# Context and latent tokens of a key or value block in one padded row, one instruction per tap of the short convolution

## The chip, the cores and the metric

The kernel runs on one core of a Trainium2 chip. The metric is the device time of one execution in microseconds (us). The time before is the median of three runs. One further execution was profiled; the rows shown below are from that one.

## The reference, cut to what matters

One layer of a hybrid backbone: a combined input projection feeds a gated DeltaNet (4 heads, 128 wide, for queries, keys and values) and a convolution module; then comes a mixture of experts. There are 1024 latent tokens and 256 context tokens. Before the DeltaNet, queries, keys and values go through a depthwise convolution over 7 tokens and a Silu. Context and latent are separate sequences for it, each padded with three zeros at both ends:

```python
def depthwise_conv_seq(x, w):
    k, ch = w.shape
    return lax.conv_general_dilated(x, w[:, None, :].astype(x.dtype), (1,), [(k // 2, k // 2)],
                                    dimension_numbers=('NWC', 'WIO', 'NWC'), feature_group_count=ch)

def delta_inputs(qkv, ba, conv_w, a_log, dt_bias):
    bsz, n, _ = qkv.shape
    qkv = jax.nn.silu(depthwise_conv_seq(qkv, conv_w)).astype(jnp.float32)
```

Queries of the context are never used by the output, so the kernel computes queries for the latent tokens alone.

## The kernel before, in words

A block is 128 channels of the projection, held with channels in the partitions and tokens along a row. There are 12 such blocks for the convolution: 0 to 3 are queries, 4 to 7 keys, 8 to 11 values. `qkv_block` (L550) makes one. It loads and splits the weights (`load_in`, L309; `split`, L290), then `fm` (L314) multiplies on TensorE into a PSUM bank of the ring "a" (4 banks): segment 0 is the 256 context tokens, segments 1 and 2 are 512 latent tokens each, 24 matmuls a segment. ScalarE copies the latent banks into the padded row `cx` (1030 wide, ring of two, L557) and, for keys and values, the context bank into a second padded row `cc` (262 wide, ring of two, L565). GpSimd writes the zeros at the ends (L554, L555, L563, L564).

`conv7` (L542) does the seven taps on a row: the first is a scaled copy on ScalarE (L546), the other six are fused multiply-adds on VectorE (L548), each of which reads the result of the one ahead of it. A key or value block calls it twice, for 1024 and for 256 columns. Keys are convolved straight into `kf`, values into `ac` (ring of two). One Silu over all 1280 columns follows (L569), then TensorE transposes ten chunks of 128 tokens (L573). For keys the squares are summed into `ssk` (L579, L580); the result goes to DRAM as `kv_d`.

What runs around it: the four key blocks come first; beside them the layer norm of the convolution module is finished (L469 to L488). Then `key_norms` (L661) needs the sums of all four key blocks. Then follow, for four pairs of chunks, `prep1` (L687: decay matrices and a product of keys, `wt`, stored to DRAM and fetched again in another layout through `bounce` into `rep`, one buffer), a value block, and `base_inverse` (L720: 15 steps, each a product `tm`, L730, and a sum `xf`, L731, on VectorE, that read `rep`). A fifth pair goes beside the query blocks. `conv_out` (L593) and `z_block` (L586) are further products; `sqq` (L766) and its matmul (L767) sum the squares of all four query blocks.

Each engine runs its own instructions in order. In this part of the program (up to L793) that order is made by the Tile framework when the program is built: it goes by the order in the source and by when it reckons an instruction to be ready, so that an engine's list mixes several blocks. From L793 on the order is planned by the kernel itself from fixed durations (`Order`, L86), and the change touches nothing there.

Of the kernel before, what the change touches and what calls it, by code (L numbers as in the profile page):

```python
# [8 lines left out]
F32 = mybir.dt.float32  # L9
# [3 lines left out]
AF = mybir.ActivationFunctionType  # L13
# [136 lines left out]
def hybrid_kernel(tc, a, out):  # L150
    nc = tc.nc
    V, S, G, PE, SY = nc.vector, nc.scalar, nc.gpsimd, nc.tensor, nc.sync
# [14 lines left out]
    def bank(tag, bufs=4, dt=F32, n=512):  # L167
        return pp.tile([128, n], dt, name=tag, tag=tag, bufs=bufs)

    def csl(c):  # L170
        return slice(c * 128, (c + 1) * 128)
# [51 lines left out]
    ident = cp.tile([128, 128], F32, name="ident")  # L223
# [15 lines left out]
    pt = bank("b")  # L239
# [69 lines left out]
    def load_in(c0):  # L309
        return load_w(win[:, :, c0:c0 + 128])  # L310
# [3 lines left out]
    def fm(wt, seg):  # L314

        t0, n = SEG[seg]
        ps = bank("a")
        for k in range(8):
            for i, (l, r) in enumerate(((wt[0], hTh), (wt[0], hTl), (wt[1], hTh))):
                PE.matmul(ps[:, :n], l[:, k, :], r[:, k, t0:t0 + n], start=(k == 0 and i == 0),  # L320
                          stop=(k == 7 and i == 2))
        return ps
# [3 lines left out]
    pt = bank("b")  # L326
# [69 lines left out]
    pt = bank("b")  # L396
# [35 lines left out]
    pt = bank("b")  # L432
# [19 lines left out]
    qf = keep2.tile([128, 4, 1024], F32, name="qf")  # L452
# [38 lines left out]
    kf = keep2.tile([128, 4, 1280], F32, name="kf")  # L491
# [37 lines left out]
    pt = bank("b")  # L529
# [10 lines left out]
    cvp = st_cv.enter_context(tc.tile_pool(name="cv", bufs=1, reuse_waits="tile"))  # L540

    def conv7(dst, src, blk, n):  # L542
        for t in range(7):
            wt = cnv[:, t * 12 + blk:t * 12 + blk + 1]
            if t == 0:
                S.activation(dst, src[:, 0:n], AF.Copy, scale=wt)  # L546
            else:
                V.scalar_tensor_tensor(dst, src[:, t:t + n], wt, dst, op0=OP.mult, op1=OP.add)  # L548

    def qkv_block(blk):  # L550
        wt = load_in(blk * 128)
        kind, h = divmod(blk, 4)
        cx = cvp.tile([128, 1030], F32, name="cx", bufs=2)
        G.memset(cx[:, 0:3], 0.0)  # L554
        G.memset(cx[:, 1027:1030], 0.0)  # L555
        for hf in range(2):
            S.activation(cx[:, 3 + hf * 512:3 + (hf + 1) * 512], fm(wt, 1 + hf), AF.Copy)  # L557
        if kind == 0:
            conv7(qf[:, h, :], cx, blk, 1024)
            S.activation(qf[:, h, :], qf[:, h, :], AF.Silu)  # L560
            return
        cc = cvp.tile([128, 262], F32, name="cc", bufs=2)
        G.memset(cc[:, 0:3], 0.0)  # L563
        G.memset(cc[:, 259:262], 0.0)  # L564
        S.activation(cc[:, 3:259], fm(wt, 0)[:, :256], AF.Copy)  # L565
        dst = kf[:, h, :] if kind == 1 else cvp.tile([128, 1280], F32, name="ac", bufs=2)
        conv7(dst[:, 256:1280], cx, blk, 1024)
        conv7(dst[:, 0:256], cc, blk, 256)
        S.activation(dst, dst, AF.Silu)  # L569
        for i0, nt in ((0, 4), (4, 4), (8, 2)):  # L570
            pt = bank("b")
            for t in range(nt):
                PE.transpose(pt[:, csl(t)], dst[:, csl(i0 + t)], ident)  # L573
            pv = pt.rearrange("p (t c) -> p t c", t=4)[:, :nt, :]
            ot = cvp.tile([128, 4, 128], F32, name="ot", bufs=2)
            if kind == 1:
                S.activation(ot[:, :nt], pv, AF.Copy)
                sq = cvp.tile([128, 4, 128], F32, name="sq", bufs=1)
                S.activation(sq[:, :nt], pv, AF.Square)  # L579
                V.tensor_reduce(ssk[:, i0:i0 + nt, h], sq[:, :nt], axis=AX.X, op=OP.add)  # L580
            else:
                V.tensor_tensor(ot[:, :nt], pv, rk[:, i0:i0 + nt, h][:, :, None].to_broadcast([128, nt, 128]),
                                op=OP.mult)
            SY.dma_start(kv_d[i0:i0 + nt, :, kind - 1, h].rearrange("t p c -> p t c"), ot[:, :nt])
# [155 lines left out]
    for h in range(4):  # L740
        qkv_block(4 + h)
    prp = st_cv.enter_context(tc.tile_pool(name="prep", bufs=1, reuse_waits="tile"))
    key_norms()
    for h in range(4):
        run_together([prep1(pairs[h])])
        qkv_block(8 + h)
        run_together([base_inverse(pairs[h])])
    for h in range(3):
        qkv_block(h)
        if h == 0:  # L750
            run_together([prep1(pairs[4])])
        if h == 1:
            run_together([base_inverse(pairs[4])])
# [7 lines left out]
    for hf in range(2):  # L761
# [8 lines left out]
        pt = bank("b")  # L770
# [1062 lines left out]
```

## Time and profile before

| | us |
|---|---|
| median of three runs | 1741.64 (1737.73 to 1743.6) |
| profiled execution | 1741.28 |
| its span in the trace | 1739.6 |
| PE busy | 1575.7 (91%) |
| DVE busy | 1001.3 (58%) |
| POOL busy | 537.5 (31%) |
| ACT busy | 494.5 (28%) |

PE is TensorE's matmuls, DVE VectorE, ACT ScalarE, POOL GpSimd, SP the queue that issues most transfers. Times in the trace count from the span's start. The blocks of the change lie between about 200 and 400 us. In the timelines an instruction's duration runs from its start until its result is there; the next instruction of the same engine can start before that, so start-to-start distances are read beside durations. "[4.18 <-DMA rep]" behind a row is idle time of the engine ahead of it and what ended it.

### The profile page before, as it was taken

The page shows a single profiled execution, that of the slowest core. Times are in us where ns is not written, and L with a number is a line of the kernel's source. Part 1 is how long each engine was busy: PE and PEld are TensorE (multiplying, and loading weights), DVE is VectorE, ACT ScalarE, POOL GpSimd, SP SyncE. Part 2 cuts the span into 40 slices and gives each one's busy share as a digit, 9 for nine tenths or more (in the row PEclk, how much of TensorE's full clock was granted, in tenths as well). Part 3 has the DMA queues.
Part 4 walks back from the last instruction along what each step waited for, and adds up shares of the span by engine and source line. Part 5 has one row for each costly group of instructions (what it writes and reads, how often), then busy time and mean ns, then how long its engine had stood idle before and what let it go on. Part 6 is the DMA issues. An engine that isn't in the chain of part 4 may idle for free. (4 is left out here: it accounts for less than half of the span.)

```text
span 1739.6 us, 23353 instructions
## 1 busy us (share of the span) xinstructions
PE 1575.7 (91%) x8348; PEld 924.7 (53%) x8348; DVE 1001.3 (58%) x2236; ACT 494.5 (28%) x1071; POOL 537.5 (31%) x486
## 2 busy tenths in 40 slices
PE   5989998876869899798999999999999999999990
PEld 1557667764647899687544434344444344433440
DVE  2488989889671886878712444444444444443425
ACT  4531266534122212444212121212121111121212
POOL 2321214543212677732011232323232222232212
PEclk8999999998889999899999999999999999999995
DMA  9455123434643334766358999999999999999956
GB/s 318 152 175 176 37 65 94 121 106 124 167 145 127 109 104 154 233 220 218 120 223 304 340 345 342 329 366 335 334 380 381 342 337 331 344 383 370 354 137 232
DMA packets 151112, 412.12 MB, mean 237 GB/s; under 512 B 19383, under 2 KB 66900, under 8 KB 125396
## 3 DMA queue, kind: packets, MB, share of 16 engines
q1 hardware_dynamic: 129994, 334.62, 53.3%
q0 software_dynamic: 18288, 67.05, 15.2%
q10 hardware_dynamic: 2714, 8.95, 1.3%
q8 instruction: 66, 1.08, 0.3%
q14 instruction: 50, 0.41, 0.1%
HBM read 339.48 MB, written 71.43 MB: 236 GB/s over the span
## 5 line engine op out<-in xcount | busy, mean ns | idle before, releaser
L1353 PE MATMUL gu<-wg,hg 128*32 128x512 f32 (+2 forms) x1968 | 463.2, 599 | 0.7 <-ACT hg L1604 0.7
L1629 DVE SCALAR_TENSOR_TENSOR ob<-dn,wc,gt2b 128x512 f32<-128x512 f32 x124 | 93.0, 750 | 366.0 <-PE dn L1373 366.0
L1638 POOL DMA_INDIRECT acc<-ob,ic x89 | 134.6, 1513 | 530.3 <-DVE st L1563 460.1
L1353 PEld LDWEIGHTS gu<-wg,hg 128*32 128x32 f32 (+2 forms) x1968 | 148.4, 137 | 203.2 <-issue 159.2
L1373 PE MATMUL dn<-wd,sg 128*32 128x512 f32 (+2 forms) x984 | 226.8, 597 | 0.5 <-ACT sg L1364 0.5
L1604 ACT ACTIVATE hg<-xt,mf 128x128 f32<-128x128 f32 x248 | 93.4, 456 | 376.4 <-PE xt L1598 375.9
L320 PE MATMUL a<-hTh,whi 128*128 128x512 f32 (+1 forms) x448 | 171.5, 383 | 3.7 <-ACT cx L557 3.7
L320 PE MATMUL a<-hTh,wlo 128*128 128x512 f32 (+1 forms) x448 | 170.3, 380 | 0.0
L320 PE MATMUL a<-hTl,whi 128*128 128x512 f32 (+1 forms) x448 | 170.3, 380 | 0.0
L1373 PEld LDWEIGHTS dn<-wd,sg 128*32 128x32 f32 (+2 forms) x984 | 77.8, 137 | 143.5 <-issue 142.7
L294 POOL TENSOR_TENSOR wlo<-wst,whi 128x512 fp32r<-128x512 f32 x56 | 82.3, 1487 | 214.3 <-ACT whi L293 209.7
L1602 DVE TENSOR_SCALAR hg<-xt,mf 128x128 f32<-128x128 f32 x248 | 84.3, 401 | 50.4 <-DMA acc<-hg 50.4
L427 DVE SCALAR_TENSOR_TENSOR ycv<-yg,cfw,ycv 128x64 f32<-128x64 f32 (+14 forms) x120 | 101.3, 844 | 6.1 <-ACT ycv L421 2.9
L320 PEld LDWEIGHTS a<-hTh,whi 128*128 128x128 f32 x448 | 84.8, 189 | 30.2 <-issue 9.9
L320 PEld LDWEIGHTS a<-hTh,wlo 128*128 128x128 f32 x448 | 85.0, 190 | 18.7 <-issue 3.4
L320 PEld LDWEIGHTS a<-hTl,whi 128*128 128x128 f32 x448 | 84.9, 189 | 18.0 <-issue 3.0
L1588 POOL DMA_INDIRECT xg<-xn_d,ig x62 | 74.1, 1195 | 64.9 <-DVE st L1583 28.3
L1552 DVE TENSOR_TENSOR oh<-posl 128x1024 bf16<-128x1024 f32 (+3 forms) x89 | 77.6, 897 | 0.0
L1598 PE MATMUL xt<-ident,xg 128*128 128x128 f32 x496 | 70.3, 285 | 0.0
L293 ACT ACTIVATE whi<-wst 128x512 fp32r<-128x512 f32 x56 | 33.0, 624 | 107.0 <-PE a L320 66.2
L1358 DVE TENSOR_TENSOR sg<-sg,gu 128x256 f32<-128x256 f32 x62 | 26.1, 421 | 63.4 <-ACT sg L1357 63.4
L1357 ACT ACTIVATE sg<-gu 128x256 f32<-128x256 f32 x62 | 23.8, 384 | 134.9 <-PE gu L1353 134.9
(433 smaller groups left out, 2488.5 us busy)
## 6 DMA issues: line engine op xcount, KB each, us to landing
wg<-exp_w_gate SPq DMA_DIRECT2D x64, 1024.0 KB
wg<-exp_w_up SPq DMA_DIRECT2D x64, 1024.0 KB
wd<-exp_w_down SPq DMA_DIRECT2D x64, 1024.0 KB
wm<-w_mod SPq DMA_DIRECT2D x24, 1024.0 KB
wst<-w_in SPq DMA_DIRECT2D x48, 256.0 KB
kv<-kv_d SPq DMA_DIRECT2D x20, 512.0 KB
rep<-bounce SPq DMA_DIRECT2D x5, 1024.0 KB
eb<-egr_d SPq DMA_DIRECT2D x18, 256.0 KB
```

Source lines behind the costliest of these rows:

```text
L294: eng.tensor_tensor(lo, st, hi.bitcast(F32), op=OP.subtract)
L320: PE.matmul(ps[:, :n], l[:, k, :], r[:, k, t0:t0 + n], start=(k == 0 and i == 0), stop=(k == 7 and i == 2))
L427: V.scalar_tensor_tensor(yc[:, lo:hi], yg[:, lo + d:hi + d], cfw[:, t * 4 + j:t * 4 + j + 1], yc[:, lo:hi], op0=OP.mult, op1=OP.add)
L1353: PE.matmul(pgu[o:o + n, :].rearrange("p (a f) -> p a f", a=2), lhsT(k, o, n), wts[r][0][:, :, k, :], start=(k == 0), stop=(k == 7), tile_ ...
L1373: PE.matmul(pd[o:o + n, :], aT[:, k, o:o + n], wts[r][1][:, k, hf * 512:(hf + 1) * 512], start=(k == 0), stop=(k == 1), tile_position=(0, ...
L1552: V.tensor_tensor(oh[:, :, o:o + n], N.iol[:, None, p0:p0 + n].to_broadcast([128, 8, n]), N.posr[:, :, r:r + 1].to_broadcast([128, 8, n]), ...
L1588: G.indirect_dma_start(out=xg, out_offset=None, in_=xn_d, in_offset=bass.IndirectOffsetOnAxis(ap=ig, axis=0))
L1598: PE.transpose(pt[:, csl(q)], nth(B['xg'][:, 0:1024], 4 * j + q, 8), ident)
L1602: V.tensor_scalar(hg[:, k, :], pt[:, csl(q)], sc_[:, k:k + 1], sh_[:, k:k + 1], op0=OP.mult, op1=OP.add)
L1604: S.activation(hg[:, k, :], pt[:, csl(q)], AF.Identity, scale=sc_[:, k:k + 1], bias=sh_[:, k:k + 1])
L1629: V.scalar_tensor_tensor(ob[:, hs_], res[hf], B['wc'], N.gt2b[:, hs_], op0=OP.mult, op1=OP.mult)
L1638: G.indirect_dma_start(out=acc_d[turn[0]], out_offset=bass.IndirectOffsetOnAxis(ap=ic[:n], axis=0), in_=B['ob'][o:o + n], in_offset=None, ...
```

## The change

For keys and values `cx` becomes one row of 1289 columns: 3 zeros, 256 context tokens, 3 zeros, 1024 latent tokens, 3 zeros. One call of `conv7` over 1283 outputs does both sequences; the three outputs in the middle are thrown away. The product of the context segment is asked for first. Keys are now convolved into `ac` (1283 wide, ring of two) as values are, and Silu writes them from there into `kf`, in two pieces. `cc` goes. Query blocks keep their instructions and use the right part of the wider row.

```diff
     def qkv_block(blk):
         wt = load_in(blk * 128)
         kind, h = divmod(blk, 4)
-        cx = cvp.tile([128, 1030], F32, name="cx", bufs=2)
-        G.memset(cx[:, 0:3], 0.0)
-        G.memset(cx[:, 1027:1030], 0.0)
+
+        cx = cvp.tile([128, 1289], F32, name="cx", bufs=2)
+        for z0 in (0, 259, 1286)[kind == 0:]:
+            G.memset(cx[:, z0:z0 + 3], 0.0)
+        if kind:
+            S.activation(cx[:, 3:259], fm(wt, 0)[:, :256], AF.Copy)
         for hf in range(2):
-            S.activation(cx[:, 3 + hf * 512:3 + (hf + 1) * 512], fm(wt, 1 + hf), AF.Copy)
+            S.activation(cx[:, 262 + hf * 512:262 + (hf + 1) * 512], fm(wt, 1 + hf), AF.Copy)
         if kind == 0:
-            conv7(qf[:, h, :], cx, blk, 1024)
+            conv7(qf[:, h, :], cx[:, 259:1289], blk, 1024)
             S.activation(qf[:, h, :], qf[:, h, :], AF.Silu)
             return
-        cc = cvp.tile([128, 262], F32, name="cc", bufs=2)
-        G.memset(cc[:, 0:3], 0.0)
-        G.memset(cc[:, 259:262], 0.0)
-        S.activation(cc[:, 3:259], fm(wt, 0)[:, :256], AF.Copy)
-        dst = kf[:, h, :] if kind == 1 else cvp.tile([128, 1280], F32, name="ac", bufs=2)
-        conv7(dst[:, 256:1280], cx, blk, 1024)
-        conv7(dst[:, 0:256], cc, blk, 256)
-        S.activation(dst, dst, AF.Silu)
+        ac = cvp.tile([128, 1283], F32, name="ac", bufs=2)
+        conv7(ac, cx, blk, 1283)
+        if kind == 1:
+            dst = kf[:, h, :]
+            S.activation(dst[:, 256:1280], ac[:, 259:1283], AF.Silu)
+            S.activation(dst[:, 0:256], ac[:, 0:256], AF.Silu)
+            chunk = [dst[:, csl(c)] for c in range(10)]
+        else:
+            S.activation(ac, ac, AF.Silu)
+            chunk = [ac[:, c * 128 + 3 * (c > 1):c * 128 + 3 * (c > 1) + 128] for c in range(10)]
         for i0, nt in ((0, 4), (4, 4), (8, 2)):
             pt = bank("b")
             for t in range(nt):
-                PE.transpose(pt[:, csl(t)], dst[:, csl(i0 + t)], ident)
+                PE.transpose(pt[:, csl(t)], chunk[i0 + t], ident)
```

## Rows read from the trace of the kernel before

**Rows 1.** Windows: us, then busy us (x instructions) by engine, clock, DMA share, GB/s.

```profile
219.00:300.00 81.00, 76.36 (x392) 58.28 (x390) 70.73 (x88) 51.29 (x81) 20.91 (x28) 1.00 0.28 85
338.00:398.00 60.00, 43.04 (x208) 35.44 (x207) 53.69 (x85) 23.46 (x38) 23.07 (x20) 0.87 0.39 105
488.00:504.00 16.00, 0.26 (x2) 0.18 (x2) 11.43 (x17) 2.94 (x5) 2.42 (x2) 0.62 0.54 143
504.00:570.00 66.00, 64.93 (x262) 46.38 (x261) 22.34 (x49) 18.36 (x30) 18.06 (x14) 0.96 0.37 123
```

**Rows 2.** Waits of DVE from 212 to 520 us, longest first.

```profile
DVE tm L730 <- DMA rep<-bounce: 23.3, 5, 8.9
DVE wt L708 <- POOL nb L707: 7.3, 4, 3.7
DVE rv L482 <- PE b L466: 5.3, 2, 2.7
DVE ssk L580 <- ACT sq L579: 4.0, 1, 4.0
```

**Rows 3.** Timelines of SP, DVE, ACT, PE: the transfers of `rep` and the last query block.

```profile
376.88 0.62 SPq L717 DMA_DIRECT2D rep<-bounce  x1
389.77 0.41 DVE L730 TENSOR_TENSOR tm<-xf,rep 128x240 f32<-128x240 f32 x1 [4.18 <-DMA rep<-bounce]
429.00 0.60 SPq L717 DMA_DIRECT2D rep<-bounce  x1
497.53 0.41 DVE L730 TENSOR_TENSOR tm<-xf,rep 128x240 f32<-128x240 f32 x1 [4.43 <-DMA rep<-bounce]
502.18 1.06 ACT L560 ACTIVATE qf<-qf 128x1024 f32<-128x1024 f32 x1 [13.01 <-DVE qf L548]
503.80 2.44 PE L767 MATMUL b<-sqq,ones 128*32 128x512 f32 x4 [15.74 <-ACT sqq L766]
```

**Rows 4.** Line L548: the DVE taps by tile, ns min/median/max, first and last start.

```profile
L548 DVE SCALAR_TENSOR_TENSOR kf<-cx,cnv,kf x24: 1271/1276/1965, 219.0 to 283.8; 128x1024 f32<-128x1024 f32 x24
L548 DVE SCALAR_TENSOR_TENSOR kf<-cc,cnv,kf x24: 467/474/1132, 220.2 to 292.5; 128x256 f32<-128x256 f32 x24
```

**Rows 5.** Timeline of DVE: taps of different chains in turn, start and duration.

```profile
236.55 1.27 DVE L548 SCALAR_TENSOR_TENSOR kf<-cx,cnv,kf 128x1024 f32<-128x1024 f32 x1
237.75 0.47 DVE L548 SCALAR_TENSOR_TENSOR kf<-cc,cnv,kf 128x256 f32<-128x256 f32 x1
238.14 1.27 DVE L548 SCALAR_TENSOR_TENSOR kf<-cx,cnv,kf 128x1024 f32<-128x1024 f32 x1
```

**Rows 6.** Timeline of DVE: taps of one chain behind each other (704, then 640).

```profile
203.21 1.87 DVE L427 SCALAR_TENSOR_TENSOR ycv<-yg,cfw,ycv 128x704 f32<-128x704 f32 x2
204.19 0.88 DVE L427 SCALAR_TENSOR_TENSOR ycv<-yg,cfw,ycv 128x640 f32<-128x640 f32 x1
```

**Rows 7.** Timeline of DVE: context taps of block 11 around a wait for `rep`.

```profile
382.39 1.51 DVE L548 SCALAR_TENSOR_TENSOR ac<-cc,cnv,ac 128x256 f32<-128x256 f32 x1
390.09 0.48 DVE L548 SCALAR_TENSOR_TENSOR ac<-cc,cnv,ac 128x256 f32<-128x256 f32 x1
393.77 0.48 DVE L548 SCALAR_TENSOR_TENSOR ac<-cc,cnv,ac 128x256 f32<-128x256 f32 x1
```

**Rows 8.** Timeline of ACT: first taps of block 4, and what follows.

```profile
214.58 1.16 ACT L546 ACTIVATE kf<-cx,cnv 128x1024 f32<-128x1024 f32 x1
215.62 0.52 ACT L546 ACTIVATE kf<-cc,cnv 128x256 f32<-128x256 f32 x1
216.02 0.64 ACT L477 ACTIVATE sql<-ycv 128x512 f32<-128x512 f32 x1
```

**Rows 9.** Timelines of ACT and POOL: the context copy of block 7 and its zeros.

```profile
268.27 0.36 ACT L565 ACTIVATE cc<-a 128x256 f32<-128x256 f32 x1
272.42 0.51 ACT L546 ACTIVATE kf<-cc,cnv 128x256 f32<-128x256 f32 x1 [3.79 <-POOL cc L564]
265.77 6.57 POOL L294 TENSOR_TENSOR wlo<-wst,whi 128x512 fp32r<-128x512 f32 x2 [12.83 <-ACT whi L293]
```

**Rows 10.** Waits of PE, 200 to 300 and 300 to 400 us.

```profile
PE b L573 <- ACT kf L569: 4.6, 2, 3.0
PE b L573 <- ACT ac L569: 16.1, 3, 9.7
```

## The prediction

> **What bounds the kernel now.** I read the windows first, to find where the change lies and which engine is full there. While the key blocks are convolved, 219 to 300 us, TensorE is busy 76.4 of 81 us and VectorE 70.7: the two are nearly level, and TensorE's idle time there is largely a wait for the Silu of a key block, which comes behind VectorE's taps (4.6 us) [rows 1, 10]. In 338 to 398 us, with value blocks and the first inverses, VectorE is busy 53.7 of 60 us and TensorE only 43.0 [rows 1]. From 504 us TensorE is full (64.9 of 66) [rows 1]: what lies behind starts when it is done, so a shift of this point goes to the end one for one, unless something fills it again.
>
> Then the waits of VectorE and, in the timelines, who ends them. The largest is the first step of an inverse waiting for `rep`: 23.3 us in five times [rows 2]. `rep` is one buffer. Its next transfer is issued when the last step of the inverse ahead of it has been read (376.88), lands for 389.77, VectorE works to the end of that inverse, and the next is issued at 429.00 [rows 3]: a ring of VectorE work and a transfer of some 13 us, in turn. The last of these waits ends at 497.53; the last taps of query block 3 stand behind it in VectorE's list, its Silu waits 13.0 us for them and starts at 502.18, and TensorE, whose next instruction is the matmul on its squares, stands 15.7 us until 503.80 [rows 3]. TensorE does nothing else meanwhile (0.26 of 16 us busy) [rows 1]. So the path to 504 us goes through VectorE's list and the transfers, not through TensorE's total. What VectorE is spared on this path counts, and only there.
>
> I looked in the same view of waits for a row in which a tap (L548) waits: there is none. The padded rows are always ready before VectorE comes to them.
>
> **The taps.** Eight key and value blocks do six taps each on VectorE, twice: 48 pairs become 48 single instructions. By durations a pair takes 1.276 + 0.474 = 1.750 us [rows 4]; a column costs (1276 - 474)/768 = 1.04 ns, so a merged tap would last 1.276 + 259 x 0.00104 = 1.545 us, 0.205 less, 9.8 us in all. But VectorE isn't held for the whole duration. In the alternating stretch the next tap starts 1.20 us after the wide one and 0.39 us after the narrow one, some 0.08 before either has ended [rows 5]. A pair holds the engine for 1.59 us, and a merged tap followed by another chain's instruction for 1.20 + 0.27 = 1.47: 0.12 saved, 6.0 us in all (0.125 unrounded).
>
> That needs the next instruction to be of another chain. Behind a tap of its own chain it starts later: in the convolution module's chain the tap of 640 columns starts 0.98 us after that of 704 [rows 6], where an uncovered 704 by [rows 5] would be 0.39 + 448 x 0.00104 = 0.86. A dependent neighbour costs 0.12 more, which is the whole saving. Before, the two chains of a block cover each other. After, cover must come from the next block, the layer norm, the sums of squares, or, with values, the steps of an inverse. These steps are a dependent chain themselves, and the context taps cover them now. So the 48 pairs save between 0 and 6.0 us; I take half cover, 0.06 a pair. Keys: 24 x 0.06 = 1.4 us, all on the path since VectorE works there with little pause. Values without block 11: 18 x 0.06 = 1.1 us, of which I count 0.5, because part of them lies ahead of waits for GpSimd and `rep` (7.3 and 23.3 us [rows 2]) that swallow it.
>
> [...]
>
> **Block 11.** Its latent taps end about 382 us. One context tap follows at 382.39; the other five, 390.09 to 393.77, stand behind an inverse's first step that waits 4.18 us for `rep` [rows 3, 7]. Merged, there are no context taps left to stand there: each latent tap gets 0.27 us longer (1.6 for six), before a wait that has 4.18 us to cover it, and five taps of 0.39 leave the stretch that ends with the issue at 429.00. That is 2.0 us on the path. It holds if the merged chain stands in the list where the latent chain does now; else it is 0.
>
> **ScalarE and GpSimd.** The first taps follow each other by 1.04 and 0.40 us [rows 8], so a column costs 0.83 ns and a merged first tap 1.04 + 0.22 = 1.26 us instead of 1.44: 0.2 x 8 = 1.4 us, off the path (ScalarE is busy 51 of 81 us [rows 1]). The Silu of a key block becomes two pieces: one more fixed part, 0.40 - 256 x 0.00083 = 0.19 us; four of them, of which the last is on the path to `key_norms`: 0.2 us against. Three zero fills in place of four on GpSimd: nothing. Keys now also pass through the ring `ac`: a block's first tap needs the Silu of the block two ahead, and the copies into `cx` (1.6 us, below) go on beside that Silu (some 1.3 us): nothing. The padded rows take 2 x (1289 + 1283) = 5144 columns, as before (2 x (1030 + 262 + 1280)): no pool moves.
>
> One stall may go or come. Block 7's context row waited 3.79 us for its zeros, which stood behind 6.57 us of weight splitting on GpSimd; VectorE was idle 4.0 us by it [rows 2, 9]. With one row the zeros of a block are written together; whether they stand behind such work is the new order's choice. Between -4.0 and +4.0 I take 0, since the work that can stand in front of them is the same.
>
> **The sum.** 1.4 + 0.5 + 2.0 - 0.2 = 3.7 us. The profiled execution took 1741.28 us (span 1739.6 and 1.7 around it), 0.36 below the median of 1741.64. 1741.28 - 3.7 = 1737.6 us; with the bounds of the cover (0 to 6.0) and of block 11 (0 or 2.0) the case reaches from 1735 to 1741.
>
> **The rivals.** *No gain*: the lone chain is exposed at every tap, and block 11's taps stay behind the wait. For it: half of today's cover is removed by the change itself. Then 0 of 6.0 and 0 of 2.0: 1741 us.
>
> *A larger gain*: every tap finds cover (6.0), block 11 (2.0, of which 0.6 is in the 6.0) and the stall on zeros goes (4.0): 11.4 - 0.2, bounded by TensorE, which in the key stage can give back only the 4.6 us it waits for Silu [rows 10]: 4.6 there, 3.0 + 1.4 behind, 0.2 against, 8.8 in all: 1732.5 us. For it speaks that TensorE also waits 16.1 us for value Silus, 9.7 of them in one go [rows 10], which an earlier block 11 shortens. Against: a new order can as well place them worse.
>
> *The full durations count*: if the fixed part were paid at every instruction, 9.8 us, 1731.5. [...]
>
> *Slower, by the refill of the row*. Now `cx` and `cc` are freed apart, and a block's latent row is refilled while its context taps run. Merged, a block keeps its whole row until its sixth tap, and two chains that take turns end nearly together. Refilling is three copies (0.40 + 2 x 0.61 by [rows 8]) and the first tap, 1.26: 2.9 us in which VectorE has only the other block's taps. It decides when that block has fewer than two taps left (2 x 1.47). Six of eight blocks need a freed row: at most 6 x 2.9 = 17 us; with half of them stalled, 9 us: 1750 us. Against: no tap waits today, and layer norm, sums and inverses can fill. A first tap also needs all three copies now, where the latent one needed two.
>
> **How the numbers follow.** About 0.3% (5.2 us, so 1736.4 and 1746.9 around the median) is what a measurement of this kernel can tell from no change. Forecast 0.42, of which 0.10 lies below 1736.4; no gain 0.12; larger gain 0.23; full durations 0.03; slower 0.20, of which 0.03 is a stall of two blocks (+5 at most). Faster: 0.10 + 0.23 + 0.03 = 0.36. Same: 0.32 + 0.12 + 0.03 = 0.47. Slower 0.17. The range 1729 to 1748 leaves out about 0.05 below (a larger gain by better order) and 0.12 above. I forecast 1737.6 us.
>
> **What would show it.** L548 on `ac` with 1283 columns, 48 times, near 1.545 us; starts 1.47 apart where another chain follows and 1.59 where it does not: their count tells the cover. VectorE's busy time falls by about 9.8 us whatever the gain is, so it proves nothing. In the waits: a row of L548 waiting for L546 is the slower rival. The last start of L767, now 503.80 [rows 3], should be near 500; if it moves and the end doesn't, the gain was given back behind it. I am wrong if the lists between 300 and 500 us come out in another order whose waits for `rep` or Silu differ by more than the taps do.

## The result, and the profile after

The changed kernel takes 1753.7 us, median of five runs (1750.01 to 1755.63), against 1741.64 for the kernel before in the same comparison: a ratio of 1.0082, with a 95% interval of 1.0062 to 1.0102. It is 12 us slower where 4 us faster was forecast, and it lies above the range. The profiled execution took 1753.7 us (span 1752.0). From `qkv_block` on, lines of the changed kernel stand 5 further down: the transposes are now L578, the squares and their sums L584 and L585, the first step of an inverse L735, the matmul on the query squares L772; the Silus of a key block are L569 and L570, the row copies L558 (context) and L560 (latent).

The taps are what was forecast: 48 of them, 1.548 us in the median.

```profile
L548 DVE SCALAR_TENSOR_TENSOR ac<-cx,cnv,ac x48: 1450/1548/2665, 223.4 to 402.9; 128x1283 f32<-128x1283 f32 x48
```

The same windows as in [rows 1] (us, then busy us by PE, PEld, DVE, ACT, POOL, then granted clock, DMA share, GB/s):

```profile
219.00:300.00 81.00, 76.18 (x378) 57.48 (x376) 66.75 (x66) 46.96 (x74) 20.63 (x22) 0.98 0.24 72
504.00:570.00 66.00, 47.48 (x185) 34.34 (x186) 39.61 (x87) 18.58 (x29) 16.71 (x13) 0.84 0.51 144
```

In the key stage VectorE is busy 66.8 of 81 us, 4.0 less than in [rows 1]. That is no gain: the stage is longer. From 504 us, where TensorE was full before (64.9 of 66), it is busy only 47.5: it still waits there for what comes late. The waits of VectorE from 212 to 520 us, against [rows 2]:

```profile
DVE tm L735 <- DMA rep<-bounce: 25.4, 4, 10.1
DVE ac L548 <- ACT ac L546: 4.5, 1, 4.5
```

The second row is new: a tap waits for a first tap. The timelines of SP, DVE, ACT and PE show the loop of `rep` and the last query block, against [rows 3]:

```profile
398.82 0.59 SPq L722 DMA_DIRECT2D rep<-bounce  x1
411.01 0.41 DVE L735 TENSOR_TENSOR tm<-xf,rep 128x240 f32<-128x240 f32 x1 [3.53 <-DMA rep<-bounce]
513.91 1.06 ACT L563 ACTIVATE qf<-qf 128x1024 f32<-128x1024 f32 x1 [6.98 <-DVE qf L548]
515.68 1.91 PE L772 MATMUL b<-sqq,ones 128*32 128x512 f32 x2 [13.07 <-ACT sqq L771]
```

The second `rep` is awaited until 411.0 in the place of 389.8, the matmul on the last query squares starts at 515.7 in the place of 503.8. So at 411 the changed kernel is already 21 us late, of which 12 are left at 515.7: the loss comes from further ahead. The key stage in the timeline of DVE:

```profile
255.54 3.14 DVE L548 SCALAR_TENSOR_TENSOR ac<-cx,cnv,ac 128x1283 f32<-128x1283 f32 x2
274.20 2.33 DVE L548 SCALAR_TENSOR_TENSOR ac<-cx,cnv,ac 128x1283 f32<-128x1283 f32 x1
279.29 16.59 DVE L548 SCALAR_TENSOR_TENSOR ac<-cx,cnv,ac 128x1283 f32<-128x1283 f32 x10
302.63 1.55 DVE L548 SCALAR_TENSOR_TENSOR ac<-cx,cnv,ac 128x1283 f32<-128x1283 f32 x1 [4.45 <-ACT ac L546]
313.13 0.41 DVE L585 TENSOR_REDUCE ssk<-sq 128x2 f32<-128x256 f32 x1
```

The stretches that these rows show are the point: between 258.7 and 274.2 us VectorE does no tap at all. Then two follow, and ten in a row, the twelve of blocks 6 and 7; both blocks end within 6 us, and their sums of squares queue up behind that until 313.1. Before, the last of these sums was at 299.4, in the timeline of DVE of the kernel before:

```profile
299.35 0.41 DVE L580 TENSOR_REDUCE ssk<-sq 128x2 f32<-128x256 f32 x1
```

Why no tap was ready is in the timeline of ACT, which fills the rows:

```profile
244.72 0.59 ACT L560 ACTIVATE cx<-a 128x512 f32<-128x512 f32 x1
270.99 0.62 ACT L560 ACTIVATE cx<-a 128x512 f32<-128x512 f32 x1
271.73 1.41 ACT L546 ACTIVATE ac<-cx,cnv 128x1283 f32<-128x1283 f32 x1
278.13 1.37 ACT L546 ACTIVATE ac<-cx,cnv 128x1283 f32<-128x1283 f32 x1
290.38 1.06 ACT L569 ACTIVATE kf<-ac 128x1024 f32<-128x1024 f32 x1 [10.88 <-DVE ac L548]
295.91 1.06 ACT L569 ACTIVATE kf<-ac 128x1024 f32<-128x1024 f32 x1 [0.44 <-DVE ac L548]
```

Block 6's first latent half is copied at 244.7 and its second only at 271.0; its first tap follows at 271.7, block 7's at 278.1. In TensorE's timeline the last of block 6's matmuls is this one, and the layer norm's matmuls (L462, L466) and those of the decay sums (L520 to L524) stand in the middle of that product, between 243.6 and 256 us:

```profile
256.77 0.39 PE L320 MATMUL a<-hTh,wlo 128*128 128x512 f32 x1
```

So the product is complete at 257.2, and its copy starts 13.8 us later: it stands behind other work in ScalarE's list (Silus and squares of key blocks, Silus of the layer norm). Both are part of the late first tap, TensorE's late product and ScalarE's list.

Last, where TensorE began to be late: its waits from 200 to 300 us.

```profile
PE b L462 <- DVE ycv L427: 5.0, 1, 5.0
```

L462 opens the layer norm, as soon as the convolution module's chain on VectorE has ended. TensorE stands 5.0 us in front of it; before it was 1.7, in TensorE's timeline of the kernel before:

```profile
212.26 1.05 PE L462 MATMUL b<-ycv,ones 128*32 128x512 f32 x2 [1.69 <-DVE ycv L427]
```

### The profile page after: what moved, and what is told of

Read it like the earlier page. It is cut to its first block, busy times and chain, and to the rows that moved or that the text cites. A ratio compares the mean times of both kernels' runs of the same rounds, so it can differ in the third digit from the quotient of the medians.

```text
span 1752.0 us, 23308 instructions
## 1 busy us (share of the span) xinstructions
PE 1582.4 (90%) x8348; PEld 932.0 (53%) x8348; DVE 994.7 (57%) x2188; ACT 495.7 (28%) x1069; POOL 541.4 (31%) x478
## 5 line engine op out<-in xcount | busy, mean ns | idle before, releaser
L320 PE MATMUL a<-hTh,whi 128*128 128x512 f32 (+1 forms) x448 | 173.2, 387 | 0.0
L320 PE MATMUL a<-hTl,whi 128*128 128x512 f32 (+1 forms) x448 | 172.0, 384 | 0.0
L320 PE MATMUL a<-hTh,wlo 128*128 128x512 f32 (+1 forms) x448 | 170.8, 381 | 0.0
L294 POOL TENSOR_TENSOR wlo<-wst,whi 128x512 fp32r<-128x512 f32 x56 | 88.6, 1601 | 232.4 <-ACT whi L293 231.0
L320 PEld LDWEIGHTS a<-hTh,whi 128*128 128x128 f32 x448 | 86.0, 192 | 27.6 <-issue 11.3
L320 PEld LDWEIGHTS a<-hTl,whi 128*128 128x128 f32 x448 | 86.2, 192 | 17.9 <-issue 3.0
L320 PEld LDWEIGHTS a<-hTh,wlo 128*128 128x128 f32 x448 | 86.0, 192 | 17.4 <-issue 1.9
L548 DVE SCALAR_TENSOR_TENSOR ac<-cx,cnv,ac 128x1283 f32<-128x1283 f32 x48 | 82.0, 1724 | 4.7 <-ACT ac L546 4.5
L617 PE MATMUL a<-whi,hcr 128*128 128x512 f32 x128 | 46.5, 444 | 20.0 <-DVE hx L618 6.6
```

What stands on the lines that cost most here:

```text
L294: eng.tensor_tensor(lo, st, hi.bitcast(F32), op=OP.subtract)
```

## The experiments

What to tell apart. ORDER, in the later texts BANK: the change also moved the context product and its copy ahead of the latent ones. In every kernel here TensorE's list has four products ahead of its wait for the convolution module's chain (96 matmuls of L320 from block 4's first to L462): block 4's three and the first of block 5. Before, that fourth one was a latent half, 24 matmuls of 512 columns; now it is the context, 24 of 256. BANK takes it that there are four because the ring "a" has four banks. The rows of the changed kernel don't bear that out (PE, then ACT):

```profile
216.50 0.80 PE L320 MATMUL a<-hTh,whi 128*128 128x512 f32 x1
207.71 0.36 ACT L558 ACTIVATE cx<-a 128x256 f32<-128x256 f32 x1
217.10 1.08 ACT L560 ACTIVATE cx<-a 128x512 f32<-128x512 f32 x2
```

Block 4's context bank is copied at 207.7, before TensorE comes to its wait (209.7), and block 5's second product starts at 216.5, ahead of every further copy. A bank was free during the wait; L462 simply stands next in the list. Why the list has four products there, no run shows. ROW: the rival on record, the refill of a merged row that is freed late. TURNS: two equal merged chains take turns and end together. COPY, TAIL and OTHER are explained where they come.

The start of L462 differs between the profiled executions by up to 3.7 us (211.0 to 214.7), and by 2.3 us even among kernels with the same four products ahead of it (211.0 in e15, 213.3 in e9), so the key stage is measured from there to the last sum of squares. All in us; "first tap" is ScalarE's for block 6, counted from the start of L462 (with two rows, the latent one):

| kernel | ratio to before (95%) | wait of L462 | first tap | last sum |
|---|---|---|---|---|
| before | 1 | 1.7 | 30.5 | 87.1 |
| changed | 1.0082 (1.0062 to 1.0102) | 5.0 | 57.1 | 98.5 |
| e1: context last | 0.9988 (0.9979 to 0.9998) | 1.7 | 36.1 | 82.3 |
| e3: before, context first | 1.0044 (1.0031 to 1.0057) | 4.8 | 47.4 | 92.0 |
| e6: changed, two calls | 1.0008 (0.9997 to 1.0019) | 5.0 | 53.7 | 90.5 |
| e7: changed, in turn | 1.0029 (1.0018 to 1.0041) | 5.0 | 57.2 | 94.0 |
| e8: context last, keys merged | 0.9988 (0.9974 to 1.0002) | 1.7 | 36.1 | 87.1 |
| e9: context last, values merged | 1.0004 (0.9988 to 1.0019) | 1.7 | 50.2 | 90.9 |
| e10: products last only | 0.9990 (0.9978 to 1.0001) | 1.7 | 36.2 | 82.0 |
| e11: copy last only | 1.0050 (1.0034 to 1.0067) | 4.7 | 58.1 | 96.3 |
| e13: block 5 last only | 0.9995 (0.9982 to 1.0008) | 2.2 | 38.0 | 82.7 |
| e16: before, block 5 first only | 1.0044 (1.0029 to 1.0058) | 4.3 | 47.3 | 93.5 |

**The order of the three products.** First the changed kernel with the old order:

```diff
-        if kind:
-            S.activation(cx[:, 3:259], fm(wt, 0)[:, :256], AF.Copy)
         for hf in range(2):
             S.activation(cx[:, 262 + hf * 512:262 + (hf + 1) * 512], fm(wt, 1 + hf), AF.Copy)
+        if kind:
+            S.activation(cx[:, 3:259], fm(wt, 0)[:, :256], AF.Copy)
```

> The changed kernel, but the context product and its copy are asked for behind the two latent ones, as before the change; row, taps and Silus stay merged. Theory ORDER (the context product went ahead, the latent columns of blocks 6 and 7 come later, and since a merged tap needs all columns both chains start late and end together): most of the loss goes, 1741 to 1746 us, and the last sum of squares of the key stage (313.1 us after the change, 299.4 before) ends between 298 and 303. Theory ROW (a merged row is freed only by its sixth tap on VectorE, so the block after next is refilled late, whichever product goes first): nothing is regained, 1751 to 1756 us, last sum near 313. Theory TURNS (two equal chains of merged taps take turns on VectorE and end together): nothing is regained either, 1750 to 1755 us.

Measured: 1735.8 us against 1738.4, ratio 0.9988, last sum at 293.5. All of the loss goes, and a little is gained, more than ORDER had put (1741 to 1746, 298 to 303). The row is as merged and as late to be freed as after the change, so ROW falls, and no tap waits for a first tap any more. In the timelines of ACT and DVE:

```profile
246.85 0.38 ACT L560 ACTIVATE cx<-a 128x256 f32<-128x256 f32 x1
247.32 1.37 ACT L546 ACTIVATE ac<-cx,cnv 128x1283 f32<-128x1283 f32 x1
266.37 1.37 ACT L546 ACTIVATE ac<-cx,cnv 128x1283 f32<-128x1283 f32 x1
293.54 0.41 DVE L585 TENSOR_REDUCE ssk<-sq 128x2 f32<-128x256 f32 x1
```

Blocks 6 and 7 start 19 us apart (6 us after the change). Block 6's last product, here the context, ends at 245.1, and its copy follows at 246.85 (L560 is the context copy here). Counted from L462, block 6's first tap is 21.0 us earlier than in the changed kernel: 8.7 of them because the last product ends earlier, the rest, some 12, in ScalarE's list. Then the order alone, in the kernel before:

```diff
         ...
         G.memset(cx[:, 1027:1030], 0.0)
+        if kind:
+            cc = cvp.tile([128, 262], F32, name="cc", bufs=2)
+            ...
+            S.activation(cc[:, 3:259], fm(wt, 0)[:, :256], AF.Copy)      # and no longer behind the latent copies
         for hf in range(2):
             S.activation(cx[:, 3 + hf * 512:3 + (hf + 1) * 512], fm(wt, 1 + hf), AF.Copy)
```

> The kernel before with one edit: the context product and its copy go ahead of the two latent ones. Two rows, twelve taps and one Silu a block stay. Theory ORDER: the order of the products costs by itself, 1746 to 1752 us, last sum of squares of the key stage at 306 to 313 us. Theories ROW and TURNS: without a merged row and merged taps the order costs little, 1739 to 1744 us, last sum near 300.

Measured: 1744.8 against 1738.4, 1.0044; the last sum at 304.8. That is between the two expectations: the order costs 6 to 8 us even with two rows (by the medians and by the ratio), with merged taps some 16 (1.0082 against 0.9988, from two comparisons).

**Which engine, and which block.** The order has two sides, TensorE's products and ScalarE's copies. Each was put back alone:

```diff
-        if kind:
-            S.activation(cx[:, 3:259], fm(wt, 0)[:, :256], AF.Copy)
-        for hf in range(2):
-            S.activation(cx[:, 262 + ...], fm(wt, 1 + hf), AF.Copy)
+        ps = [fm(wt, 1 + hf) for hf in range(2)]      # e10; e11: pc = fm(wt, 0), and its copy last
+        if kind:
+            S.activation(cx[:, 3:259], fm(wt, 0)[:, :256], AF.Copy)
+        for hf in range(2):
+            S.activation(cx[:, 262 + ...], ps[hf], AF.Copy)
```

> The changed kernel with the context product behind the two latent ones on TensorE, but the context copy still ahead of the latent copies in what ScalarE is asked. It tells apart by which engine the order costs. Theory BANK (TensorE: with the context product ahead, the fourth bank of the ring holds a product of 24 x 256 in the place of 24 x 512, TensorE runs out of work some 3 us before the convolution module's chain ends, and block 6's last latent product falls behind the layer norm's matmuls): wait of L462 for ycv back from 5.0 to about 1.7 us, last sum at 293 to 299 us, 1735 to 1741 us. Theory COPY (ScalarE's list puts the latent copies last, so the first tap of a merged row waits): last sum at 306 to 313 us, 1747 to 1754 us.

> The mirror image of the run with the products alone reordered: the changed kernel with the context product first on TensorE as after the change, and only the context copy behind the latent copies in what ScalarE is asked. Theory BANK (the order of TensorE's products is the whole cost): no help, wait of L462 for ycv at 4.8 to 5.0 us, last sum of squares at 306 to 314 us, 1746 to 1755 us. Theory COPY: 1736 to 1742 us.

Measured: 1736.7 us (0.9990) and 1747.9 us (1.0050). The products decide. Whether the asked order of the copies has a small part in it stays open: 1.0050 lies below the 1.0082 of the changed kernel, but the two come from different comparisons and their intervals touch. Next, the old order for block 5 alone, the block whose first product is the fourth ahead of the wait:

```diff
-        if kind:
+        if kind and blk != 5:
             S.activation(cx[:, 3:259], fm(wt, 0)[:, :256], AF.Copy)
         ...
+        if blk == 5:
+            S.activation(cx[:, 3:259], fm(wt, 0)[:, :256], AF.Copy)
```

> The changed kernel with the old order (context product and copy last) for block 5 alone; blocks 4, 6, 7 and all values keep the context product first. Block 5's first product is what the fourth bank holds while TensorE waits for the convolution module's chain. Theory BANK, first half (what counts is the run-ahead before 212 us): wait of L462 for ycv back to 1.7 to 2.5 us, block 6 complete some 3 us earlier or more, last sum at 296 to 306 us, 1738 to 1748 us. Theory of every block (each block's late latent columns cost by themselves): 1750 to 1754 us, last sum at 308 to 313 us.

Measured: 1739.3 us against 1739.6, 0.9995, last sum at 294.4: one block of eight carries the loss, to within the intervals. Its mirror image, the kernel before with the context first for block 5 alone (the edit of the run above, under `if blk == 5`):

> The kernel before (two rows, twelve taps), with the context product and copy first for block 5 alone: the mirror image of the changed kernel with the old order for block 5. Theory BANK: block 5's first product is what the fourth bank holds in front of the wait for the convolution module's chain; 24 matmuls of 256 columns start 0.120 us apart, of 512 columns 0.227 us, so 2.6 us of work less lie ahead, and the wait of L462 goes from 1.7 to 4.3 us or, with what the lower clock behind it costs, some 5; last sum of squares 90 to 93 us behind the start of L462 (87.1 in the kernel before, 92.0 with the context first in every block), 1741 to 1746 us. If every block's order counts: 87 to 88 us, 1737 to 1740 us.

Measured: 1745.0 against 1737.8, 1.0044, as with the context first in every block. The first rows of L462 in TensorE's timeline, of block 5 last (e13) and of the mirror image (e16):

```profile
211.72 1.37 PE L462 MATMUL b<-ycv,ones 128*32 128x512 f32 x2 [2.20 <-DVE ycv L427]
```

```profile
213.55 1.89 PE L462 MATMUL b<-ycv,ones 128*32 128x512 f32 x2 [4.27 <-DVE ycv L427]
```

The 4.27 is the old wait of 1.69 and the 2.6 us of matmuls that are missing ahead of it. So the cause is shown from both sides: four products stand ahead of the wait, and the change made the fourth the smallest one, block 5's context. What follows from it is seen, not tested by itself: the work left of block 5 is larger, and the lists that the framework makes come out in another order. On TensorE the layer norm's matmuls on its squares (L462), the L466 behind them and the decay sums stand within block 6's last product, where in e1 most of them come behind it (that product ends at 257.2 in the changed kernel, at 245.1 in e1); on ScalarE the copy of that product waits 13.8 us in the place of 1.8.

**Why merged taps pay more for it.** The taps of the changed kernel were split again, row and order kept:

```diff
-        conv7(ac, cx, blk, 1283)
+        conv7(ac[:, 259:1283], cx[:, 259:1289], blk, 1024)
+        conv7(ac[:, 0:259], cx[:, 0:265], blk, 259)
```

> The changed kernel with its one row, its order of products and its Silus, but each tap is two instructions again (1024 columns and 259), so that only the merging of taps is taken back. Theory ORDER as far as it needs merged taps, and theory TURNS (a merged chain waits for all columns, and two merged chains end together): 1742 to 1747 us. Theory ROW (the refill of the shared row, freed only when both of its parts are done): stays at 1751 to 1757 us, with the 12 taps of 1.20 and 0.39 us in the place of 6 of 1.55, a tenth of a us slower a pair of taps.

Measured: 1740.1 against 1738.4, 1.0008: nearly all of the loss goes, more than expected (1742 to 1747), though the wait of L462 stays at 5.0. Context taps need only the context copy. Eight of them, the last of block 5 and the first of block 6, run in the stretch in which a merged chain had nothing to do, ahead of block 6's first latent tap, which starts at 266.79 as the last of the second row's four (timeline of DVE):

```profile
262.88 2.07 DVE L548 SCALAR_TENSOR_TENSOR ac<-cx,cnv,ac 128x259 f32<-128x259 f32 x5
265.48 2.59 DVE L548 SCALAR_TENSOR_TENSOR ac<-cx,cnv,ac 128x259 f32<-128x259 f32 x4
268.31 1.94 DVE L548 SCALAR_TENSOR_TENSOR ac<-cx,cnv,ac 128x1024 f32<-128x1024 f32 x1
```

The row was as shared as after the change, against ROW once more. And with the merged chains forced to follow each other:

```diff
+                if t == 1 and last_tap:
+                    tc.add_manual_dep(ins.ins, last_tap[-1].ins.name, ...)   # behind the last tap of the key block ahead
```

> The changed kernel with one more rule for the order of VectorE's list: the second tap (the first of VectorE) of a block stands behind the last tap of the key block ahead of it, so that two chains never take turns. Dependent taps in a row start 1.59 us apart where alternating ones start 1.47 us apart, some 1 us for a block. Theory TURNS: block 6 ends by 285 us and its transposes and sums lie beside the taps of block 7; last sum of squares at 300 to 305 us in the place of 313, time 1742 to 1747 us. Theory ORDER: the latent columns come late all the same, so 1750 to 1755 us. Theory ROW: an earlier end of one block frees its row earlier, 1746 to 1750 us.

Measured: 1744.4 against 1738.4, 1.0029; the stage is 94.0 us long in the place of 98.5. So taking turns is a part of the price. In the key stage it is 4.5 of the 11.4 us, and the first tap of block 6 is as late as ever; the last sum at 307.6 missed TURNS' 300 to 305. In the time it is more: 1744.4 lies in TURNS' range (1742 to 1747), and from 1.0082 to 1.0029 some 9 of the 14 us are regained. The rule also puts the value and query taps behind block 7's last one; whether the rest of the 9 us comes from there, no run shows.

**Where the gain of the taps goes.** With the order put right the key stage is 4.8 us shorter than before (82.3 against 87.1), but only some 2 us reach the end. Keys and values merged apart, both with the context last:

```diff
+        if kind == 1:      # e8; e9: kind == 2
             conv7(ac, cx, blk, 1283)
+        else:
+            conv7(ac[:, 259:1283], cx[:, 259:1289], blk, 1024)
+            conv7(ac[:, 0:259], cx[:, 0:265], blk, 259)
```

> Row, ring and Silus as after the change, context product asked for last; only the taps of the four key blocks are merged, those of the value blocks are two instructions each (1024 and 259 columns). With all taps merged and this order the last sum of squares ended at 293.5 us (299.4 before the change) and the time was 0.9988 of before. If the keys carry that gain: last sum at 293 to 295 us, 1735 to 1737 us. If the values carry it: last sum as here, but the time 1738 to 1741 us.

> As the run with merged key taps alone, the other way round: context product last, the taps of the value blocks merged, those of the key blocks two instructions each. If the keys carry the gain: last sum of squares at 298 to 301 us, 1738 to 1741 us. If the values carry it: 1735 to 1737 us. If neither can be told (what the key stage gives is swallowed by the waits for rep and by TensorE behind it): both runs within 2 us of before.

Measured: 0.9988 and 1.0004, with intervals that overlap. The times don't tell which half carries the 2 us, and the key stage was short only with both merged (87.1 and 90.9 here): in e8 eight taps of block 8 stand ahead of block 7's last sum, in e1 three. This question stays open. Where the rest goes is in the first inverse steps and the waits of VectorE in e1, against [rows 2, 3]:

```profile
376.43 0.41 DVE L735 TENSOR_TENSOR tm<-xf,rep 128x240 f32<-128x240 f32 x1 [2.35 <-DMA rep<-bounce]
434.78 0.41 DVE L735 TENSOR_TENSOR tm<-xf,rep 128x240 f32<-128x240 f32 x1 [6.19 <-DMA rep<-bounce]
468.44 0.41 DVE L735 TENSOR_TENSOR tm<-xf,rep 128x240 f32<-128x240 f32 x1 [11.19 <-DMA rep<-bounce]
DVE tm L735 <- DMA rep<-bounce: 31.2, 5, 11.2
DVE ssk L585 <- ACT sq L584: 1.0, 2, 0.7
```

The second `rep` is there 13.3 us earlier than before (376.4 against 389.8), but the waits for `rep` grow from 23.3 to 31.2 us, and by the matmul on the query squares (502.5 against 503.8) 1.3 us are left. To see whether that place is worth anything, the last inverse's first step was put behind the last tap of query block 3, in e1's kernel and in the kernel before:

```diff
-        if h == 1:
-            run_together([base_inverse(pairs[4])])
     run_together([conv_out(0)])
     qkv_block(3)
+    run_together([base_inverse(pairs[4])])      # and its first product behind query block 3's last tap
```

> Merged taps with the context product asked for last, and the last inverse's first step set behind the last tap of query block 3 in VectorE's list. It asks where the 5.8 us that the key stage gives with merged taps go. Theory TAIL (the taps of query block 3 behind the wait for rep, and TensorE's 12.0 us wait for the squares of that block, set the stage's end, so what is gained ahead of them fades in the wait): the matmul on the squares starts near 493 us in the place of 502.5, and with TensorE full behind it some 5 to 9 us come through: 1727 to 1732 us. Theory OTHER (another wait takes the place of this one, conv_out's for one, or TensorE's work behind 504 us is regained anyway): within 2 us of the run without this rule, 1734 to 1738 us.

> The kernel before (two rows, twelve taps) with the same rule: the last inverse's first step behind the last tap of query block 3. Against the run with merged taps and the same rule it shows what merging is worth when this wait is gone. Theory TAIL: 1730 to 1735 us here, and the merged one 2 to 6 us below it. Theory OTHER: 1736 to 1741 us, and the difference to the merged one stays at the 2 us that it is with the wait.

Measured: 1729.7 us (0.9951, 0.9934 to 0.9968) with merged taps and 1734.5 (0.9974, 0.9963 to 0.9985) without, against 1738.5. In the timelines of DVE, ACT and PE of the first (its lines stand 2 to 6 further down than in the changed kernel):

```profile
489.51 7.00 DVE L550 SCALAR_TENSOR_TENSOR qf<-cx,cnv,qf 128x1024 f32<-128x1024 f32 x4
496.54 1.06 ACT L566 ACTIVATE qf<-qf 128x1024 f32<-128x1024 f32 x1 [4.81 <-DVE qf L550]
498.29 0.41 DVE L738 TENSOR_TENSOR tm<-xf,rep 128x240 f32<-128x240 f32 x1 [1.78 <-DMA rep<-bounce]
498.65 2.43 PE L778 MATMUL b<-sqq,ones 128*32 128x512 f32 x4 [6.91 <-ACT sqq L777]
```

The four taps lie in front of the wait, which is 1.8 us now, and the matmul starts at 498.7, not at 493 as TAIL put it; some 4 to 6 us come through to the end in either kernel. So TAIL holds, smaller than put. What merging is worth without this wait was to be 2 to 6 us. The medians say 4.9 and the ratios 4, but their intervals touch, and in the two profiled executions the matmul starts at 498.65 and 498.48: it isn't settled. The first of the two is the fastest kernel of the study.

## Why the prediction was wrong, step by step

**The step that failed is a term that the sum doesn't have.** The section on the change says that the context product is asked for first; the prediction prices taps, Silus, zeros and rings, and of this move it says only that a first tap now needs all three copies. So the move was put at nothing, without a reason. It issues 24 matmuls past 48 others on TensorE. Its price could be read before the change: matmuls of 512 columns start 0.227 us apart, of 256 columns 0.120, in the kernel before as after it (TensorE's timeline of the changed kernel):

```profile
206.18 0.39 PE L320 MATMUL a<-hTl,whi 128*128 128x512 f32 x1
206.41 0.39 PE L320 MATMUL a<-hTh,wlo 128*128 128x512 f32 x1
206.63 0.28 PE L320 MATMUL a<-hTh,whi 128*128 128x256 f32 x1
206.75 0.28 PE L320 MATMUL a<-hTl,whi 128*128 128x256 f32 x1
```

So 24 x 0.107 = 2.6 us less work lies ahead of a wait that was 1.7 us already. The mirror image measured 4.3. The forecast would have had to take these 2.6 us, in a stage where TensorE is busy 76 of 81 us [rows 1], as lost, and more if the lists behind it come out worse. In the runs the move cost 6 to 8 us with two rows (e3, e16) and some 16 with merged taps (changed against e1).

**The taps themselves were right.** 1.545 us forecast, 1.548 measured. In e1's timeline of DVE a tap followed by another chain's instruction holds the engine 1.46 us (263.00 to 264.46), and two of one chain in a row end 3.14 us after the first start, so 1.59 apart; forecast were 1.47 and 1.59.

```profile
217.98 3.14 DVE L548 SCALAR_TENSOR_TENSOR ac<-cx,cnv,ac 128x1283 f32<-128x1283 f32 x2
263.00 1.55 DVE L548 SCALAR_TENSOR_TENSOR ac<-cx,cnv,ac 128x1283 f32<-128x1283 f32 x1
264.46 0.68 DVE L585 TENSOR_REDUCE ssk<-sq 128x4 f32<-128x512 f32 x1
```

The rival by which the full durations count doesn't hold for the tap at 263.00: its neighbour starts 1.46 us behind its start, 0.09 us ahead of its end.

**The sum of 3.7 us** lies at the upper edge of what the order put right gives: 0.9988 is 2.1 us, with an interval of 0.3 to 3.7. That it comes so near is luck, for how it is made up doesn't fit. Keys were to give 1.4 us and the key stage gave 4.8; of these 3.0 are the wait of a sum for its squares, which the prediction had left at 0 between -4.0 and +4.0 (4.0 in [rows 2], 1.0 in e1). Block 11's 2.0 and the values' 0.5 can't be found at the end; the waits for `rep`, named as what swallows part of them, took 7.9 us more.

**The slower rival** gave the right side and the right sign, for a reason that is wrong in the main. The row of waits that was named as its mark is there (4.5 us), two chains that take turns do end together, and that costs (e7). But the row wasn't refilled late because it was freed late: e1 keeps the row and has neither. So its 1750 us, near the 1753.7, were luck. (Of its terms, the 0.61 us of a latent copy doesn't stand in [rows 8]; in the traces such a copy takes 0.6 us.)

**Two other sentences held.** VectorE's busy time proves nothing: it fell by 6.6 us in the slower kernel. And "I am wrong if the lists between 300 and 500 us come out in another order" was the right kind of warning, but named the wrong stretch: the order turned at 243 to 271 us, because of the product that stood ahead of the wait at 210. A loss in the key stage went to the end nearly whole (the stage 11.4 us longer, the kernel 12 slower; in e11 9.2 and 9; smaller ones lie between 3.4 and 1 in e6 and 4.9 and 8 in e3), a gain there did not (4.8 and 2): what is early waits for `rep` (31.2 us in e1, 23.3 before), what is late makes `rep` late (awaited until 411.0 in the changed kernel, 389.8 before).

## What to carry to other kernels

When an edit moves the place where an operand is asked for, price its producers first: count the matmuls that pass each other, and look in the timeline at which product the list places last ahead of TensorE's next wait. Here a larger product in that place shortened the wait by about as much as it took longer itself (2.6 us longer; the wait 4.3 us in e16, 1.7 in the kernel before). And an instruction that joins two inputs starts when the later one is there: in the changed kernel block 6's latent halves were copied at 244.7 and 271.0, and its merged first tap started at 271.7. Merging, worth some 2 us in e1, did not pay for that wait (the changed kernel is 12 us slower), so see who fills the engine meanwhile.

## What the runs showed of the hardware

Behind a wait of 5.0 us (changed kernel) TensorE's granted clock was 0.50, behind one of 1.7 us (e1) it was 1.00. Windows of the wait for L462 and of what follows, changed kernel, then e1 (columns as above; the clock stands ahead of the DMA share):

```profile
209.70:214.60 4.90, 0.00 (x0) 0.00 (x0) 4.65 (x9) 0.00 (x0) 4.34 (x13) 0.70 0.42 107
214.60:217.00 2.40, 2.34 (x3) 0.68 (x4) 2.14 (x16) 0.39 (x1) 0.00 (x0) 0.50 0.00 0
```

```profile
209.60:211.20 1.60, 0.00 (x0) 0.00 (x0) 1.49 (x5) 0.00 (x0) 1.49 (x10) 1.00 0.28 83
211.20:213.20 2.00, 1.94 (x6) 0.83 (x7) 2.00 (x16) 0.86 (x2) 0.00 (x0) 1.00 0.00 0
```

Within the 4.9 idle us the clock fell (0.70 is the mean); behind them the granted clock is 0.50, and the first two matmuls take 1.91 us; behind 1.6 idle us it stays at 1.00 and they take 1.04. In e13, behind 2.2 idle us, it was 0.63 in the mean of the next 2.3 us, and the loss was gone all the same: the clock adds to the price (0.9 us at the first two matmuls), it isn't the cause.

Some taps beside GpSimd last longer. In the changed kernel 11 of the 48 merged taps take 1.99 us or more, and each of the 11 overlaps a GpSimd instruction; of the 37 others (1.73 us at most) 11 do too. What tells them apart is who was first: all 11 long ones start while a GpSimd instruction is already running, nine of the 11 others start ahead of it, and two in its last 0.4 us. One of the long ones in the timelines of DVE and POOL:

```profile
308.82 2.33 DVE L548 SCALAR_TENSOR_TENSOR ac<-cx,cnv,ac 128x1283 f32<-128x1283 f32 x1
308.31 1.49 POOL L699 TENSOR_TENSOR rr<-Li,gg 128x512 fp32r<-128x512 f32 x1
```

A context tap of 0.48 us took 1.51 in the kernel before [rows 7]. The largest addition is 1.0 to 1.1 us at each width: 0.47 to 1.52 with 256 columns and 1.28 to 2.31 with 1024 in the kernel before, 1.55 to 2.67 with 1283. Each of these three longest taps starts while a GpSimd instruction is running. What in the chip makes such a tap longer, no run here shows.
